# A mixture-of-experts block on one core: the third-largest expert gets 64 slots and whole weights, and its chunks alternate with the second split expert's

## The chip, the cores and the metric

The kernel runs on one core of a Trainium2 chip, the other cores being idle. The metric is the device time of one execution in microseconds (us), as the median of several runs. Five engines work side by side, each through its own queue in order: TensorE (PE in the profile; its weight loads are PEld), VectorE (DVE), ScalarE (ACT), GpSimd (POOL) and SyncE (SP), which here issues the loads from memory.

## The reference, cut to what matters

The program is a network of two layers over 256 tokens. Only the end of the second layer is touched: a mixture of eight experts, two chosen for each token.

```python
D_MODEL = 1024; SEQ = 256; N_EXPERTS = 8; TOP_K = 2; D_FF_EXPERT = 3584

def swiglu(h, w1, w3, w2):
    return (jax.nn.silu(h @ w1) * (h @ w3)) @ w2

def moe_swiglu(h, router, w1, w3, w2):
    logits = (h @ router).astype(jnp.float32)
    top_v, top_i = lax.top_k(logits, TOP_K)
    gates = jax.nn.softmax(top_v, axis=-1)
    dense_gate = jnp.sum(jax.nn.one_hot(top_i, N_EXPERTS, dtype=jnp.float32) * gates[..., None], axis=-2).astype(h.dtype)
    out = jnp.zeros_like(h)
    for e in range(N_EXPERTS):
        out = out + dense_gate[..., e:e + 1] * swiglu(h, w1[e], w3[e], w2[e])
    return out
```

All is float32. The weights of the eight experts are 352 MB and are read once from memory.

## The kernel before

**Places and slots.** The kernel numbers the experts by places p: place 0 is expert 0, places 1 to 7 are the other seven from the largest count of tokens to the smallest. `CAPS` gives each place its slots: 128, 192, 128, 128, 64, 64, 64, 64. Tokens beyond a place's slots would be worked off in a loop at the end of `moe`, which runs as often as there is an overflow.

**Chunks.** The 3584 hidden columns of an expert are cut into seven chunks of 512. A job (p, c) is one chunk c of place p. It has a first stage (`stage_a`), which multiplies the gathered tokens with a chunk of w1 and w3, a transposing step (`stage_t`, through PSUM bank `bk_po`), and a second stage (`stage_b`), which multiplies with a chunk of w2. The second stage of a job is written behind the first stage of the next one. A chunk uses six weight tiles of 128 x 2048 float32 (1 MB): four in its first stage, two in its second. The list `jobs` sets the order: all chunks of places 0, 2 and 3, then those of places 4 to 7, among which the seven chunks of place 1 are spread.

**Split and whole weights.** For places 0 to 3 a tile is split after it has landed: ScalarE copies it into a rounded half `hi` (L269) and VectorE subtracts that from the raw tile to get `lo` (L270). The tokens are split in the same way, and each product is three matmuls in the fast mode: hi by hi, hi by lo, lo by hi (L1554 to L1556). That gives 48 matmuls in a first stage and 24 in a second; below, such a chunk is called split. For places 4 to 7 the raw tile is used as it is, in float32, with 64 slots on one half of the array's columns, and two such matmuls run side by side on the two halves (L1551, L1763); these chunks are called whole, with 16 and 8 matmuls. The profile lists each of these matmuls as two. The results of a whole first stage lie in two halves of a PSUM bank, which ScalarE copies and VectorE adds (L1704 to L1709).

**Outputs.** A place's second stages add up in two PSUM banks over all seven chunks (`main`, bank `bk_mm`). Place 1, whose chunks are spread, uses two fresh banks for each block of slots and each chunk, and VectorE adds them up in SBUF, in the unused part of `xT` (`ysp`, L1860). At the last chunk `finish` scales the output and queues four scatter steps (L1815, L1816, bank `bk_ada`).

**Helper steps.** `prep_b`, `prep_c` and `prep_d` gather the tokens of later places, eight gather steps each (L1526). They and the scatter steps stand in a list `fills`, from which `stage_a` takes one after each weight tile.

**Loads.** Eleven slots of one tile each serve raw tiles and both halves of split ones. `plan` holds the loads in the order of use, `fetch` issues one (L1412, on SyncE's queue), `loaded` holds the raw tiles, `ready` those that were split or need no split. `prime` loads until `LEADS` (five in the steady state) tiles are in `loaded` and moves one on to `ready`, splitting it where it has to be; `next_w` calls it while `ready` holds no more than one tile. The instructions are then put in order by a scheduler, engine by engine, by the priority in which they were written and by what it thinks is free; the wait for a slot is part of that.

Of the kernel before, what the change touches and what calls it, by code (L numbers as in the profile page):

```python
# [10 lines left out]
F32 = mybir.dt.float32  # L11
# [7 lines left out]
P = 128  # L19
D = 1024  # L20
KD = 8
# [44 lines left out]
    return arrs, where  # L66


CAPS = (128, 192, 128, 128, 64, 64, 64, 64)
_CT, _CW = _const_tables()  # L70


# [95 lines left out]
def tile_backbone(ctx: ExitStack, tc: tile.TileContext, A, out, upto=99, dbg=None):  # L168
# [8 lines left out]
    AHEAD, LEAD, NWT, PRE, SPL = 1, 4, 11, (1, 3, 5, 7), (1, 3)  # L177
# [18 lines left out]
    def bank(tag="mm"):  # L196
        if turn and tag == "ax":
            turn.append(turn.pop(0))
            tag = turn[0]
        return ps[0].tile([P, 512], F32, tag=tag, name="bk_" + tag, bufs=NB[tag])  # L200
# [1207 lines left out]
    def load2(src, whole, parts=1):  # L1408
        raw = wtile(F32)
        dst, src = [a.rearrange("p (a b c) -> p a b c", a=2, b=parts) for a in (raw, src)]  # L1410
        for i in range(parts):
            nc.sync.dma_start(dst[:, :, i, :], src[:, :, i, :])  # L1412
        return raw, whole
# [12 lines left out]
    def prime():  # L1426
        lead[0] += 1
        n = LEADS[min(lead[0], len(LEADS) - 1)]
        while plan and len(loaded) < n:
            fetch()  # L1430
        ready.append(split2(*loaded.pop(0), SPC if lead[0] < NSPC else 2048))

    def next_w():
        while len(ready) <= AHEAD and (loaded or plan):
            prime()
        return ready.pop(0)

# [8 lines left out]

    jobs = []
    job = 0
    for p in (0, 2, 3, 4, 5, 6, 7):
        for c in range(7):  # L1450
            jobs.append((p, c))
            if p >= 4:
                if job in (1, 5, 9, 13, 17, 20, 23):
                    jobs.append((1, sum(j[0] == 1 for j in jobs)))
                job += 1
    ws = {}

    def w_get(p):
        if p not in ws:
            ws[p] = w_of(p)  # L1460
        return ws[p]

    for n in range(len(jobs) + 1):
        if n < len(jobs):
            for i in range(4):
                plan.append(lambda p=jobs[n][0], c=jobs[n][1], i=i: load2(w_get(p)[0](c, i), p >= 4))
        if n:
            for q in range(2):
                plan.append(lambda p=jobs[n - 1][0], c=jobs[n - 1][1], q=q, n=n: load2(w_get(p)[1](c, q), p >= 4,
                                                                                 2 if n == len(jobs) else 1))  # L1470

    def moe(mp, dw, oh0):
# [35 lines left out]
        def xg128():  # L1508
            return Pair(mp.tile([P, 2, KD, P], F32R, tag="xg", name="xg", bufs=4))
# [161 lines left out]
        def prep(specs, blocks, later):  # L1671
            oh = mk_oh(specs)
            ohT = mk_ohT(oh, specs)
            for k in range(KD):
                if later:
                    fills.append(lambda k=k: gather_k(oh, blocks, k))
                else:
                    gather_k(oh, blocks, k)
            return ohT
# [145 lines left out]
        def spec(p, base=0.0, gi=None, io=iota):  # L1825
            return (io, col(slp, p), base, col(gtp, p), p if gi is None else gi)


        def prep_b():
            xs[2], xs[3] = xg128(), xg128()  # L1830
            ohTs[2], ohTs[3] = prep([spec(2), spec(3)], [xs[2], xs[3]], True)

        def prep_c(a):
            t = mp.tile([P, 2, KD, 64], F32, tag="xg", name="xf", bufs=4)
# [8 lines left out]
        main = {}  # L1843

        def stage_2(p, c, gT):
            if p != 1:
                if c == 0:
                    main[p] = [[bank(), bank()]]
                stage_b(gT, main[p], c == 0, c == 6)
                if c == 6:  # L1850
                    finish(main[p][0], p, ohTs[p], p == 7)
                return
            acc = [[bank("ax"), bank("ax")] for _ in range(2)]
            stage_b(gT, acc, True, True)
            for b in range(2):
                for half in range(2):
                    if c == 0:
                        V.tensor_copy(ysp[b][half], two(acc[b][half]))
                    else:
                        V.tensor_tensor(ysp[b][half], ysp[b][half], two(acc[b][half]), op=ALU.add)  # L1860
            if c == 6:
                finish(ysp[0], 1, ohTs[1])
                finish(ysp[1], 8, ohTs[8])

        prev = None
        gT = []
        for p, c in jobs:
            if (p, c) == (0, 1):
                ohTs[0], = mk_ohT(oh0, [spec(0)])
                prep_b()  # L1870
            if (p, c) == (2, 1):
                prep_c(4)
            if (p, c) == (2, 3):
                prep_d()
            if (p, c) == (3, 1):
                prep_c(6)

            def mid():
                if prev is not None:
                    gT.append(stage_t(prev[1]))  # L1880

            gl = stage_a1(*a0) if prev is None else stage_a([xs[1], xs[8]] if p == 1 else [xs[p]], mid)
            if prev is not None:
                stage_2(*prev[0], gT.pop())
            prev = ((p, c), gl)
# [95 lines left out]
```

## Time and profile before

| | us |
|---|---|
| median of 3 runs | 2097.13 |
| lowest, highest | 2096.21, 2103.83 |
| profiled execution | 2096.44 |
| its span, first to last instruction | 2094.7 |
| busy: PE, PEld, DVE, ACT (whole span) | 2026.0, 1438.0, 1288.0, 906.0 |
| moved from memory | 493.4 MB |

The experts take the span from about 1123 us to its end. The profile comes from one execution; its times are us from the span's start. A busy share is an average over stages with different limits, so the stage has to be looked at by itself: there, the start of one matmul after another tells how long a piece takes (the listed duration of one overlaps with the next), and the idle time in square brackets at the end of a row, with the arrow, tells what the engine waited for.

### The profile page before, as it was taken

Reading aid. Unit: us, or ns where it says so; the run is one execution under the profiler, and the core shown is the slowest. Engines: PE = TensorE matmul, PEld = TensorE weight load, DVE = VectorE, ACT = ScalarE, POOL = GpSimd, SP = SyncE. Lnnn points to the kernel's source line nnn. Section 1 sums busy time; section 2 is a strip of 40 time slices with the busy share of each in tenths; the row PEclk is TensorE's granted clock in tenths of the full one; section 3 lists DMA queues with packets and bytes.
Section 4 is the critical chain, followed back from the end, with each engine's and each line's share of the span. In section 5 each row is a group of like instructions: output and inputs, shape, how many; then the busy total and the mean of one; then the engine's idle time right before and its main releaser. Section 6 shows DMA issues by size and latency. Waiting matters only on the chain. (4 is left out here: it accounts for less than half of the span.)

```text
span 2094.7 us, 26701 instructions
## 1 busy us (share of the span) xinstructions
PE 2026.0 (97%) x10170; PEld 1438.0 (69%) x10170; DVE 1288.0 (61%) x1878; ACT 906.0 (43%) x1296; POOL 109.1 (5%) x148
## 2 busy tenths in 40 slices
PE   7999999889999999999999999999999999999997
PEld 4776756688777878888888888878654554545453
DVE  5366557777566664765477888887644344434443
ACT  4346525643222223544356776767532232232322
POOL 0000015600000000100101000000000000000000
PEclk9999999999999999999999999999999999999998
DMA  8422432025444674322254999999989999999994
GB/s 317 150 94 96 151 121 95 24 68 161 142 150 151 209 236 128 125 61 81 84 228 146 337 364 323 322 334 335 371 352 397 401 406 398 390 418 383 384 361 181
DMA packets 89445, 496.25 MB, mean 237 GB/s; under 512 B 10080, under 2 KB 10848, under 8 KB 46048
## 3 DMA queue, kind: packets, MB, share of 16 engines
q1 hardware_dynamic: 89312, 494.49, 64.3%
q8 instruction: 82, 1.34, 0.3%
q14 instruction: 51, 0.42, 0.1%
HBM read 493.40 MB, written 1.05 MB: 236 GB/s over the span
## 5 line engine op out<-in xcount | busy, mean ns | idle before, releaser
L270 DVE TENSOR_TENSOR w<-w 128x2048 fp32r<-128x2048 f32 (+1 forms) x186 | 384.5, 2081 | 58.7 <-ACT w L269 40.9
L269 ACT ACTIVATE w<-w 128x2048 fp32r<-128x2048 f32 (+1 forms) x186 | 320.5, 1748 | 62.2 <-DVE w L270 35.4
L269 ACT ACTIVATE whi<-raw 128x1024 fp32r<-128x1024 f32 x151 | 160.0, 1060 | 404.1 <-PE bk_mm L298 263.3
L270 DVE TENSOR_TENSOR wlo<-raw,whi 128x1024 fp32r<-128x1024 f32 x151 | 186.6, 1236 | 140.8 <-ACT whi L269 138.3
L297 PE MATMUL bk_mm<-fH,whi 128*128 128x512 f32 (+1 forms) x360 | 140.0, 390 | 2.0 <-DVE xT L518 1.2
L299 PE MATMUL bk_mm<-fH,wlo 128*128 128x512 f32 (+1 forms) x360 | 138.8, 387 | 2.1 <-DVE wlo L270 2.1
L297 PE MATMUL bk_mm<-hH,whi 128*128 128x512 f32 (+1 forms) x384 | 137.5, 361 | 2.2 <-ACT hH L269 2.2
L298 PE MATMUL bk_mm<-fL,whi 128*128 128x512 f32 (+1 forms) x360 | 139.2, 388 | 0.0
L298 PE MATMUL bk_mm<-hL,whi 128*128 128x512 f32 (+1 forms) x384 | 136.2, 355 | 0.0
L299 PE MATMUL bk_mm<-hH,wlo 128*128 128x512 f32 (+1 forms) x384 | 135.5, 354 | 0.0
L1551 PE MATMUL bk_pt<-w,xf 128*64 128x512 f32 x448 | 113.0, 601 | 0.0
L1704 ACT COPY g<-bk_ax 64x512 f32<-64x512 f32 x35 | 20.4, 582 | 207.9 <-PE bk_ax L1551 207.7
L1551 PE MATMUL bk_ax<-w,xf 128*64 128x512 f32 x448 | 107.2, 597 | 0.0
L1763 PE MATMUL bk_mm<-w,gf 128*64 128x512 f32 x448 | 105.3, 597 | 0.0
L1555 PE MATMUL bk_ax<-w,xg 128*128 128x512 f32 x224 | 90.6, 405 | 7.2 <-DVE w L270 7.2
L1554 PE MATMUL bk_ax<-w,xg 128*128 128x512 f32 x224 | 89.6, 400 | 0.0
L1555 PE MATMUL bk_pt<-w,xg 128*128 128x512 f32 x220 | 88.5, 402 | 0.4 <-DVE w L270 0.2
L1556 PE MATMUL bk_ax<-w,xg 128*128 128x512 f32 x224 | 88.8, 396 | 0.0
L456 POOL TENSOR_TENSOR rstd<-rstd,mhalf 128x2 f32<-128x2 f32 (+2 forms) x11 | 10.3, 937 | 1496.1 <-DVE rstd L455 1477.0
L1554 PE MATMUL bk_pt<-w,xg 128*128 128x512 f32 x220 | 88.2, 401 | 0.0
L1556 PE MATMUL bk_pt<-w,xg 128*128 128x512 f32 x220 | 87.5, 398 | 0.0
L297 PEld LDWEIGHTS bk_mm<-hH,whi 128*128 128x128 f32 x384 | 71.8, 188 | 21.8 <-issue 5.4
(568 smaller groups left out, 4357.4 us busy)
## 6 DMA issues: line engine op xcount, KB each, us to landing
w<-in_m SPq DMA_DIRECT2D x334, 1024.0 KB, 7.6
raw<-in_f SPq DMA_DIRECT2D x66, 512.0 KB, 3.7
araw<-in_adc SPq DMA_DIRECT2D x56, 512.0 KB, 3.9
araw<-in_ada SPq DMA_DIRECT2D x32, 512.0 KB, 7.2
raw<-in_evx SPq DMA_DIRECT2D x29, 512.0 KB, 3.7
raw<-in_odx SPq DMA_DIRECT2D x22, 512.0 KB, 3.6
raw<-in_evo SPq DMA_DIRECT2D x12, 512.0 KB, 3.7
xT<-in_xt SPq DMA_DIRECT2D x4, 1024.0 KB, 6.4
```

Of the source, the lines that this page charges most:

```text
L269: a = S.activation(hi, src, AF.Copy)
L270: v = V.tensor_tensor(lo, src, hi.bitcast(F32), op=ALU.subtract)
L297: T.matmul(o, wh, xh, start=first, stop=False)
L298: T.matmul(o, wh, xl, start=False, stop=False)
L299: T.matmul(o, wl, xh, start=False, stop=last)
L456: G.tensor_tensor(r, r, mhalf[:, :n], op=ALU.pow)
L1551: T.matmul(o[c:c + 64], sl(b[0]), wh, start=k < 2, stop=k >= K - 2, tile_position=(0, c))
L1554: T.matmul(o, sl(b[0]), wh, start=first, stop=False)
L1555: T.matmul(o, sl(b[0]), wl, start=False, stop=False)
L1556: T.matmul(o, sl(b[1]), wh, start=False, stop=last)
L1704: S.copy(g[0:64], hb[b][0][64:128])
L1763: T.matmul(accs[0][half][64 * q2:64 * q2 + 64], gT[0][0][:, f, :], wh[:, hs], start=first and q == 0, stop=last and q == 1, tile_position= ...
```

## The change

Place 3 gets 64 slots and whole weights (`p >= 3` in `load2`, `spec` with `iotd`, a float32 token tile of 64 columns). Its chunks no longer follow those of place 2 but alternate with them, chunk by chunk. Its output adds up in SBUF as that of place 1 does, in the first block of `ysp`, which is free until place 1 begins. The gathers of places 6 and 7 (`prep_c(6)`) start at job (4, 1). `prime` now counts the tiles in `ready` too (six in all), and `next_w` goes on past whole tiles, up to four, until a split tile is in `ready`, so that a split can be written up to four tiles ahead of its use.

```diff
-CAPS = (128, 192, 128, 128, 64, 64, 64, 64)
+CAPS = (128, 192, 128, 64, 64, 64, 64, 64)
...
     def prime():
         lead[0] += 1
         n = LEADS[min(lead[0], len(LEADS) - 1)]
-        while plan and len(loaded) < n:
+        while plan and (not loaded or len(loaded) + max(len(ready), 1) < n + 1):
             fetch()
         ready.append(split2(*loaded.pop(0), SPC if lead[0] < NSPC else 2048))
 
     def next_w():
-        while len(ready) <= AHEAD and (loaded or plan):
+        while (len(ready) <= AHEAD or len(ready) < 4 and not any(w[1] is not None for w in ready)) and (loaded or plan):
             prime()
         return ready.pop(0)
...
-    for p in (0, 2, 3, 4, 5, 6, 7):
+    for p in (0, 2, 4, 5, 6, 7):
         for c in range(7):
             jobs.append((p, c))
+            if p == 2:
+                jobs.append((3, c))
...
-                plan.append(lambda p=jobs[n][0], c=jobs[n][1], i=i: load2(w_get(p)[0](c, i), p >= 4))
+                plan.append(lambda p=jobs[n][0], c=jobs[n][1], i=i: load2(w_get(p)[0](c, i), p >= 3))
...
         def prep_b():
-            xs[2], xs[3] = xg128(), xg128()
-            ohTs[2], ohTs[3] = prep([spec(2), spec(3)], [xs[2], xs[3]], True)
+            xs[2], xs[3] = xg128(), [mp.tile([P, KD, 64], F32, tag="xg", name="xf", bufs=4)]
+            ohTs[2], ohTs[3] = prep([spec(2), spec(3, io=iotd)], [xs[2], xs[3]], True)
...
         def stage_2(p, c, gT):
-            if p != 1:
+            if p not in (1, 3):
...
-            acc = [[bank("ax"), bank("ax")] for _ in range(2)]
+            acc = [[bank("ax"), bank("ax")] for _ in gT]
             stage_b(gT, acc, True, True)
-            for b in range(2):
+            for b in range(len(gT)):
...
             if c == 6:
-                finish(ysp[0], 1, ohTs[1])
-                finish(ysp[1], 8, ohTs[8])
+                for b in range(len(gT)):
+                    finish(ysp[b], (p, 8)[b], ohTs[(p, 8)[b]])
...
-            if (p, c) == (3, 1):
+            if (p, c) == (4, 1):
                 prep_c(6)
```

The order of VectorE before, in one chunk of place 3 (`w` are weight tiles with their buffer number: `lo<-raw,hi`; `gl` is the lower half of the transposed hidden chunk, L1701 the product for the next one):

```order
L1701 TENSOR_TENSOR g_12233<-g_12233,bk_pt_12151 128x512
L270 TENSOR_TENSOR w_12239<-w_12152,w_12238 128x2048
L270 TENSOR_TENSOR w_12257<-w_12170,w_12256 128x2048
L270 TENSOR_TENSOR gl_12326<-bk_po_12320,gh_12325 128x512
L270 TENSOR_TENSOR w_12277<-w_12197,w_12276 128x2048
L270 TENSOR_TENSOR w_12305<-w_12215,w_12304 128x2048
L270 TENSOR_TENSOR w_12332<-w_12236,w_12331 128x2048
L270 TENSOR_TENSOR w_12350<-w_12254,w_12349 128x2048
```

The order of VectorE now, from the end of a first stage of place 2 through the chunk of place 3 that follows (the lines of the changed kernel lie two further on: L1703, L1743 for L1701, L1741):

```order
L1703 TENSOR_TENSOR g_11558<-g_11558,bk_pt_11482 128x512
L1862 TENSOR_TENSOR xT_72<-xT_72,bk_ax_11561 128x2x256
L1862 TENSOR_TENSOR xT_72<-xT_72,bk_pt_11562 128x2x256
L1707 TENSOR_TENSOR g_11612<-g_11612,bk_ax_11577 64x512
L270 TENSOR_TENSOR gl_11601<-bk_po_11595,gh_11600 128x512
L270 TENSOR_TENSOR w_11588<-w_11569,w_11587 128x2048
L1710 TENSOR_TENSOR g3_11613<-g3_11613,bk_pt_11578 64x512
L1711 TENSOR_TENSOR g_11612<-g_11612,g3_11613 64x512
L1743 COPY gf_11703<-bk_po_11698 128x256
L270 TENSOR_TENSOR w_11627<-w_11579,w_11626 128x2048
L270 TENSOR_TENSOR w_11645<-w_11585,w_11644 128x2048
```

The six subtractions of a pair of chunks stand as one (`w_11588`, the first tile of place 2's second stage) and five behind `gf` (`w_11627` is the second tile, `w_11645` the first of the next first stage); before, each pair had twelve.

The order of TensorE before, in the second stage of a chunk of place 3, at the change from its first tile (`w_12217`, `w_12218`) to its second (`w_12238`, `w_12239`):

```order
L1555 MATMUL bk_mm_11691<-w_12218,gh_12193 128x512
L1556 MATMUL bk_mm_11691<-w_12217,gl_12194 128x512
L1554 MATMUL bk_mm_11690<-w_12238,gh_12193 128x512
L1554 MATMUL bk_mm_11691<-w_12238,gh_12193 128x512
L1738 MATMUL bk_po_12320<-ca_67,g_12233 128x128 x4
L1555 MATMUL bk_mm_11690<-w_12239,gh_12193 128x512
L1556 MATMUL bk_mm_11690<-w_12238,gl_12194 128x512
```

And now, in the second stage of a chunk of place 2, at the same change of tiles:

```order
L1557 MATMUL bk_mm_10556<-w_11588,gh_11600 128x512
L1558 MATMUL bk_mm_10556<-w_11587,gl_11601 128x512
L1740 MATMUL bk_po_11698<-ca_67,g_11612 128x64 x4
L1556 MATMUL bk_mm_10555<-w_11626,gh_11600 128x512
L1556 MATMUL bk_mm_10556<-w_11626,gh_11600 128x512
L1557 MATMUL bk_mm_10555<-w_11627,gh_11600 128x512
L1558 MATMUL bk_mm_10555<-w_11626,gl_11601 128x512
```

The transposes of place 3's chunk now stand between the two tiles, and what VectorE needs from them (`gf`) stands ahead of the subtraction that gives `w_11627`.

The order of TensorE now, in a first stage of place 2 just behind its first tile (`w_11644`, `w_11645`):

```order
L1558 MATMUL bk_ax_11660<-w_11644,xg_9496 128x512
L1556 MATMUL bk_ax_11660<-w_11664,xg_9496 128x512
L1765 MATMUL bk_ax_11740<-w_11642,gf_11703 64x512
L1557 MATMUL bk_ax_11660<-w_11665,xg_9496 128x512
L1558 MATMUL bk_ax_11660<-w_11664,xg_9496 128x512
```

Matmuls of place 3's second stage (L1765) are set in among those of place 2's first: one here, two behind the second tile, five at the end. Before, no second stage was cut up in this way in the chunks of places 2 and 3.

## Rows read from the trace of the kernel before

**Rows 1.** Windows: length; busy us by engine; PEclk, DMA share, GB/s.

```profile
1243.60:1506.30 262.70, 261.15 (x1211) 210.72 (x1210) 219.89 (x156) 182.06 (x162) 0.00 (x0) 1.00 0.94 335
1506.30:1538.60 32.30, 31.81 (x136) 13.97 (x134) 14.30 (x20) 12.79 (x13) 0.00 (x0) 1.00 1.00 413
1538.60:2069.00 530.40, 516.06 (x2318) 265.43 (x2316) 224.44 (x266) 151.45 (x170) 0.00 (x0) 1.00 0.95 384
```

**Rows 2.** Waits of PE, 1243.6 to 1506.3: total us, times, longest.

```profile
PE bk_ax L1555 <- DVE w L270: 1.2, 2, 0.6
```

**Rows 3.** Timeline of PE, one split chunk: start, us, engine, line, operation, tiles.

```profile
1226.28 0.40 PE L1554 MATMUL bk_ax<-w,xg 128*128 128x512 f32 x1
...
1237.52 0.63 PE L1554 MATMUL bk_mm<-w,gh 128*128 128x512 f32 x2
...
1243.58 0.39 PE L1554 MATMUL bk_ax<-w,xg 128*128 128x512 f32 x1
```

**Rows 4.** Timeline of PE, one whole chunk and the next one's start.

```profile
1660.30 3.65 PE L1551 MATMUL bk_ax<-w,xf 128*64 128x512 f32 x16
1663.89 0.46 PE L1738 MATMUL bk_po<-ca,g 64*128 64x64 f32 x4
1664.28 3.65 PE L1551 MATMUL bk_pt<-w,xf 128*64 128x512 f32 x16
1667.76 3.60 PE L1763 MATMUL bk_mm<-w,gf 128*64 128x512 f32 x16
1671.19 1.89 PE L1551 MATMUL bk_ax<-w,xf 128*64 128x512 f32 x8
```

**Rows 5.** Timeline of PE, single whole matmuls among split ones.

```profile
1497.79 1.07 PE L1551 MATMUL bk_ax<-w,xf 128*64 128x512 f32 x2
1498.79 0.51 PE L1555 MATMUL bk_pt<-w,xg 128*128 128x512 f32 x1
...
1504.84 1.08 PE L1551 MATMUL bk_ax<-w,xf 128*64 128x512 f32 x4
1505.85 0.50 PE L1555 MATMUL bk_mm<-w,gh 128*128 128x512 f32 x1
```

**Rows 6.** Timeline of all engines, a whole chunk ahead of place 1's second stage.

```profile
1643.95 0.66 PE L1738 MATMUL bk_po<-ca,g 128*128 128x128 f32 x4
...
1644.54 1.93 PE L1551 MATMUL bk_pt<-w,xf 128*64 128x512 f32 x6
...
1645.40 0.63 ACT L1706 ACTIVATE g<-g 64x512 f32<-64x512 f32 x1
...
1647.18 1.90 ACT L269 ACTIVATE w<-w 128x2048 fp32r<-128x2048 f32 x1
...
1649.11 2.29 DVE L270 TENSOR_TENSOR w<-w 128x2048 fp32r<-128x2048 f32 x1 [1.37 <-ACT w L269]
...
1651.46 0.50 PE L1555 MATMUL bk_ax<-w,gh 128*128 128x512 f32 x1 [0.98 <-DVE w L270]
```

**Rows 7.** Timeline of all engines, from transposes over `gf` to a subtraction.

```profile
1615.33 0.43 PE L1738 MATMUL bk_po<-ca,g 64*128 64x64 f32 x4 [0.49 <-DVE g L1709]
...
1615.68 1.08 PE L1763 MATMUL bk_mm<-w,gf 128*64 128x512 f32 x4
1615.79 0.42 DVE L1741 COPY gf<-bk_po 128x256 f32<-128x256 f32 x1 [0.61 <-PE bk_po L1738]
1616.13 2.28 DVE L270 TENSOR_TENSOR w<-w 128x2048 fp32r<-128x2048 f32 x1
```

**Rows 8.** DMA, 1500 to 2070, in 40 slices; issues, KB each, median us to landing.

```profile
GB/s 380 408 372 225 423 333 423 418 419 420 360 412 421 416 367 420 342 421 419 418 420 316 415 420 421 417 420 350 423 403 368 290 415 420 314 420 325 405 419 194
...
w<-in_m SPq DMA_DIRECT2D x206, 1024.0 KB, 10.2
```

**Rows 9.** Waits of PE, 1538.6 to 2069: total us, times, longest.

```profile
PE bk_ax L1555 <- DVE w L270: 10.9, 12, 2.1
```

**Rows 10.** The additions in SBUF, by source line: ns min, median, max.

```profile
L1860 DVE TENSOR_TENSOR xT<-xT,bk_ax x12: 678/683/690, 1658.8 to 2029.7; 128x512 f32<-128x512 f32 x12
```

## What the change will do to the time: a prediction

> **What bounds the kernel now.** I began with the table of stretches. From 1243.6 to 1506.3 us the chunks of the second split expert (p = 2) and then of the third-largest (p = 3) run; in these 262.7 us TensorE is busy for 261.2, while the loads move 335 GB/s [rows 1]. The waits of TensorE there come to 1.2 us in two places [rows 2]. So this stretch is bound by TensorE's own work, and the copies, subtractions and loads stand behind it. A split chunk without helper steps takes 17.30 us: 11.24 for the 48 matmuls of its first stage and 6.06 for the 24 of its second with four transposes (1226.28, 1237.52, 1243.58) [rows 3]. Fourteen make 242.2, which leaves 20.5 us for the 32 helper steps of the stretch (4 + 4 scatter steps of `finish`, 8 + 8 + 8 gathers of `prep`): 0.64 us each. In the last stretch the loads are nearly the bound too: 384 GB/s over 530 us [rows 1], against 420 in its best slices [rows 8]; a tile of 1.049 MB then takes 2.50 us. The clock is full in all three stretches [rows 1].
>
> **The third-largest expert with 64 slots.** Its 55 tokens fit: counted from the reference's inputs the router gives the eight experts 87, 39, 55, 145, 15, 52, 18 and 101, and 55 is the third behind expert 0, so the overflow loop stays empty. A whole chunk needs 7.46 us for the first stage with its transposes (1660.30 to 1667.76) and 3.43 for the second (to 1671.19) [rows 4], 10.9 in place of 17.3: 6.4 saved per pair of chunks if nothing else moved. Its 42 tiles also need no copy (1.90) and no subtraction (2.29) [rows 6]; these were hidden behind TensorE and are worth nothing by themselves. The output now adds two VectorE operations of 0.68 per chunk [rows 10]; VectorE was busy for 219.9 of 262.7 [rows 1] and loses 42 subtractions, so they hide.
>
> **One pair of chunks, by the new order.** Between the first matmul of one p = 2 chunk and the next, TensorE now runs: 48 split matmuls, 11.24; inserted into them, whole matmuls of the p = 3 second stage, first one alone, then two, at the end five. One alone takes 1.00 (1497.79 to 1498.79), two 1.01 (1504.84 to 1505.85) [rows 5]; five are three turns of 0.86 (3.43 / 4), 2.58. With 0.1 for each way back that is 4.9 where eight together took 3.43. Then the whole first stage, 7.46, whose transposes are the larger ones here (0.59 in place of 0.39 [rows 4, 6]), 7.66; then the split second stage, 6.06 with 0.35 in place of 0.44 for its transposes [rows 3, 7], and 0.15 to change over. Sum: **29.9**. Loads for 12 tiles need 30.0 at best, no more than this.
>
> Two waits come on top, both read from the order of VectorE and ScalarE. (1) The split of the first second-stage tile stands behind ScalarE's silu of the whole chunk. In rows 6 the same sequence runs: from the start of the transposes (1643.95) the silu ends after 2.08 (1645.40 + 0.63); a copy and subtraction follow, 1.93 to the subtraction's start and 2.35 more until TensorE goes on (1647.18, 1649.11, 1651.46): 6.4 in all. TensorE arrives after 0.59 + 3.48 (second half of the whole stage) + 0.15 + 0.47 (two matmuls that need the copy alone): 4.7. **Wait 1.7.** (2) The subtraction of the second tile stands behind `gf`, which needs the transposes that TensorE does between the two tiles. From their start to the split's it is 0.80 (1615.33, 1615.79, 1616.13) [rows 7], and 2.35 until TensorE goes on: 3.15. TensorE is there after 0.35 + 0.47. **Wait 2.3.** Behind the waiting matmul all of TensorE's queue stands still. The other four subtractions follow at 2.3 each, faster than the 2.8 of the 12 matmuls that use one; no third wait. The slots for the loads free early enough: the first raw tile of the next pair is issued when the third split tile is used up, some 17 us before its copy. So a pair takes **33.9 us, against 34.6 before**: seven pairs save 4.9, not 45. Bounds for a pair: 30.0, if both waits vanish, and 38.4, if copy and subtraction (1.93 + 2.35) are exposed in full twice. I take 33.9, since both sequences stand in the rows.
>
> **Helper steps.** Twenty of the 32 remain in the stretch, 20 x 0.64 = 12.8. In four places the order puts such steps, or the next expert's whole matmuls, exactly where wait (2) is, and that fills 4 x 2.3 = 9.2. The first pair has expert 0's last split second stage instead of a whole one, 6.06 for 4.9: 1.2 more, and single whole matmuls stand among split ones, about 3 (three of 1.00, an estimate from rows 5). 12.8 + 1.2 + 3 - 9.2 = 7.8 in place of 20.5: **12.7 saved**. Twelve steps move behind 1506.3 (gathers of the last two experts, scatter of p = 2): +7.7; the last p = 3 second stage is whole now, -2.6; three of the gathers stand where the first p = 1 chunk made TensorE wait for a split, up to 2.1 [rows 9], -1.6: **+3.5**.
>
> **The chunks of the largest expert (p = 1), seven of them.** Their first stage is now cut by one and by three whole matmuls, about 1.4 more each. Against that, the split of their first second-stage tile moves ahead of the transposes' `gl` on VectorE, which removes a wait of about 1.2 (one half of the 10.9 us in 12 waits [rows 9] and the gap before 1651.46 [rows 6]), and one set of transposes goes from among the whole matmuls to the split ones, 0.5. Net -0.3 x 7 = **-2**, with ends of -7 (all waits of rows 9 gone) and +8 (the cuts cost, nothing is won, as the loads hold the stretch).
>
> **Sum.** -4.9 - 12.7 + 3.5 - 2 = -16.1. The profiled execution took 2096.4 (span 2094.7 and 1.7 around it), so 2080.3; the median of the three runs shown is 0.7 higher: **2081**.
>
> **Rivals.** (a) *The loads eat it.* With the second stretch shorter, everything rests on the last one, where loads run at 384 of 420 GB/s: the steps moved there cost in full (+2.6 and +1.6) and p = 1 comes out at +8 in place of -2: 2081 + 14 = 2095. For it: a long landing time, 10.2 us in the middle [rows 8]. Against it: TensorE's waits there are for VectorE [rows 9], not for a load.
> (b) *Slower.* Copy and subtraction are exposed in full at both places of every pair, because the slot of the copied half or the raw tile is not there when ScalarE's turn comes: 38.4 per pair, 31 more in seven; the four filled places give back some 8: 2104. It takes over from the kernel before at 36.2 per pair. Against it: in rows 6 the copy starts as soon as ScalarE is free.
> (c) *The earlier splitting does what its rule says* (up to four tiles ahead, past whole ones) and neither wait appears: 30.0 per pair, bound by the loads, 27 less; the filled places then win nothing, +9: 2063. Against it: the order, where the subtraction stands behind `gf`.
> (d) *Loads capped lower.* Twelve tiles would then set the pair. The slices of 420 GB/s and the mean of 384 over 530 us speak against any cap below [rows 1, 8]. The Trainium skill, "DMA: Bandwidth & Descriptors", section "Where 436 GB/s comes from", lets the memory side bind such loads at about 358 GB/s per core; by that a pair would take 12.58 MB / 358 = 35.1, and seven some 8 more: 2089. Here one core runs alone, and the trace exceeds that figure; the measurement decides.
>
> **How the numbers follow.** About 0.5% (10.5 us) is what a measurement of this kernel can tell from no change. Chances: the forecast 0.50, with a spread of its own of 2072 to 2091, three quarters of it below 2086.6; (a) 0.26; (b) 0.11; (c) 0.10; (d) 0.03. Faster: 0.38 + 0.10 = 0.48; slower: 0.11; the same: 0.41. The range must take in half of (c) and stop before (b): 2064 to 2100 leaves out about 2 in 10.
>
> **What would show it.** Right: the distance between first matmuls of two p = 2 chunks is 33 to 35 us without helper steps; in each pair TensorE waits twice for VectorE's subtraction, for about 1.7 and 2.3; loads in the stretch run near 370 GB/s. Wrong: waits of 4 at these places (b); waits on loads, or landing times over 10 us in the second stretch (a, d); no waits and 30 us (c). If the last stretch changes by more than 8 us, the p = 1 term was mis-sized.

## The result: slower by 0.9%, and where the time went

The changed kernel takes 2118.31 us (median of 5 runs, 2115.46 to 2121.98) against 2097.13 of before (median of 5): ratio 1.0088, 95% interval 1.0074 to 1.0103. The forecast was 2081, with a range from 2064 to 2100; the time moved the other way.

The stretches of the changed kernel, cut at the first matmul of each chunk of place 2, then at the first and the last chunk of place 1 (columns as in [rows 1]: length; busy us by engine; PEclk, DMA share, GB/s):

```profile
1238.97:1280.57 41.60, 39.89 (x177) 26.34 (x176) 26.43 (x27) 19.48 (x22) 0.00 (x0) 0.96 0.82 315
1280.57:1324.61 44.04, 39.44 (x170) 23.51 (x169) 22.57 (x27) 18.23 (x26) 0.00 (x0) 0.93 0.73 286
1324.61:1366.15 41.54, 36.50 (x150) 21.46 (x148) 20.96 (x24) 16.65 (x21) 0.00 (x0) 0.91 0.77 304
1366.15:1400.92 34.77, 31.38 (x134) 17.67 (x133) 19.10 (x16) 14.77 (x14) 0.00 (x0) 1.00 0.91 362
1400.92:1436.04 35.12, 31.73 (x130) 17.76 (x128) 18.78 (x15) 14.98 (x12) 0.00 (x0) 0.97 0.90 359
1436.04:1472.46 36.42, 33.03 (x130) 18.81 (x129) 18.51 (x14) 14.74 (x12) 0.00 (x0) 0.93 0.87 346
1472.46:1546.64 74.18, 69.75 (x297) 32.85 (x295) 33.07 (x47) 19.09 (x29) 0.00 (x0) 1.00 0.89 354
1546.64:2007.72 461.08, 446.27 (x1972) 228.19 (x1972) 187.53 (x215) 133.80 (x153) 0.00 (x0) 0.99 0.94 377
```

The same two stretches of the kernel before, from the first matmul of (2, 0) to that of (1, 0) and from there to (1, 6):

```profile
1243.58:1538.65 295.07, 293.03 (x1345) 224.71 (x1343) 234.19 (x176) 194.88 (x175) 0.00 (x0) 1.00 0.95 343
1538.65:1985.25 446.60, 435.29 (x1963) 224.35 (x1961) 186.34 (x214) 130.20 (x144) 0.00 (x0) 1.00 0.96 391
```

Of the changed kernel's rows, the first six are pairs of chunks. Only the fourth looks like the forecast of 33.9; the first three, which hold the helper steps (but for one gather in the fourth), take over 41, and five of the six have a PEclk below 1, where [rows 1] had 1.00 throughout. By stretch, in us:

| stretch | before | forecast | after |
|---|---|---|---|
| start to the first matmul of (2, 0) | 1243.6 | 1243.6 | 1239.0 |
| (2, 0) to (1, 0) | 295.1 | 281.0 | 307.7 |
| (1, 0) to (1, 6) | 446.6 | 444.6 | 461.1 |
| (1, 6) to the end of the span | 109.5 | 109.5 | 108.4 |

The forecast column takes -4.9 - 12.7 + 3.5 off the second stretch and 2 off the third. What lies ahead of (2, 0) differs by up to 7 us between profiled executions, also where this part is written the same (1245.0 and 1238.0 in the two kernels e3 and e14 below), so from here on times are counted from (2, 0). From there the change costs 26.0 us, of which 12.6 come before (1, 0), 14.5 between (1, 0) and (1, 6), and -1.1 after.

The waits of TensorE, 1118 to 2090 us (total us, times, longest):

```profile
PE bk_mm L1557 <- DVE w L270: 14.8, 10, 2.1
PE bk_po L1740 <- DVE g L1711: 5.4, 11, 0.5
PE bk_ax L1557 <- DVE w L270: 4.5, 7, 1.6
PE bk_ada L1528 <- DVE xs1b L1542: 4.0, 3, 1.3
PE bk_mm L1765 <- DMA w<-in_m: 3.5, 3, 1.2
PE bk_ada L1528 <- ACT xf L1538: 3.3, 6, 0.6
```

The largest row before, over the same stretch:

```profile
PE bk_ax L1555 <- DVE w L270: 12.1, 14, 2.1
```

The first row of the changed kernel is new and is the two waits of the forecast: the second stages of place 2 (`bk_mm`) wait for VectorE's subtraction. The gathers (`bk_ada`, L1528), which had no row of this kind before, now wait for their own evacuation, and whole second stages of the last stretch wait for a load. The six rows come to 35.5 us, the longest wait to 2.1.

In the fourth pair, which has the full clock of 2.4 GHz (PEclk 1.00), ScalarE, VectorE and TensorE at the two places:

```profile
1388.48 1.90 ACT L269 ACTIVATE w<-w 128x2048 fp32r<-128x2048 f32 x1
...
1390.41 2.29 DVE L270 TENSOR_TENSOR w<-w 128x2048 fp32r<-128x2048 f32 x1 [1.86 <-ACT w L269]
...
1392.76 0.50 PE L1557 MATMUL bk_mm<-w,gh 128*128 128x512 f32 x1 [1.34 <-DVE w L270]
...
1395.79 0.42 DVE L1743 COPY gf<-bk_po 128x256 f32<-128x256 f32 x1 [1.78 <-PE bk_po L1740]
1396.13 4.48 DVE L270 TENSOR_TENSOR w<-w 128x2048 fp32r<-128x2048 f32 x2
...
1398.47 0.50 PE L1557 MATMUL bk_mm<-w,gh 128*128 128x512 f32 x1 [2.05 <-DVE w L270]
```

The copy (behind the silu) ends, the subtraction follows, TensorE goes on after a wait of 1.34; then `gf`, the next subtraction and a wait of 2.05. The forecast had 1.7 and 2.3.

In the second pair, TensorE through two gather steps and the second stage behind them, with three rows of ScalarE and VectorE:

```profile
1314.65 0.74 PE L1528 MATMUL bk_ada<-oh,hTok 128*128 128x256 f32 x4 [0.78 <-DVE ohT L1664]
1315.42 0.37 ACT L1538 ACTIVATE xg<-bk_ada,mod 128x128 fp32r<-128x128 f32 x1 [6.09 <-PE bk_ada L1528]
...
1315.88 1.91 ACT L269 ACTIVATE w<-w 128x2048 fp32r<-128x2048 f32 x1
...
1316.72 0.71 PE L1528 MATMUL bk_ada<-oh,hTok 128*128 128x256 f32 x4 [1.33 <-DVE xs1b L1542]
1317.83 2.29 DVE L270 TENSOR_TENSOR w<-w 128x2048 fp32r<-128x2048 f32 x1 [1.25 <-ACT w L269]
1317.85 0.99 PE L1556 MATMUL bk_mm<-w,gh 128*128 128x512 f32 x2 [0.42 <-ACT w L269]
1320.17 0.79 PE L1557 MATMUL bk_mm<-w,gh 128*128 128x512 f32 x1 [1.34 <-DVE w L270]
1320.77 0.63 PE L1558 MATMUL bk_mm<-w,gl 128*128 128x512 f32 x1
1321.19 0.63 PE L1557 MATMUL bk_mm<-w,gh 128*128 128x512 f32 x1
...
1324.61 0.57 PE L1556 MATMUL bk_ax<-w,xg 128*128 128x512 f32 x1
```

A gather's results are taken out of PSUM by ScalarE and then by VectorE (L1538, L1542). In ScalarE's queue that stands ahead of the copy of a second-stage tile: ScalarE is idle for 6.09 us until the gather comes, and copies the tile only then, at 1315.88. TensorE waits four times: 0.78 ahead of the first gather, 1.33 until VectorE has taken out its result, 0.42 for the copy and 1.34 for the subtraction. Then the clock is at its lower level, 1.2 GHz: matmuls start 0.42 apart (0.23 in the fourth pair), and from the wait to the next stage the piece takes 4.44 us (1320.17 to 1324.61) where the same piece in the fourth pair takes 2.45 (1398.47 to the next stage at 1400.92).

### The profile page after: what moved, and what is told of

It reads as the page before. It is cut to its first block, busy times and chain, and to the rows that moved or that the text cites. A ratio compares the mean times of both kernels' runs of the same rounds, so it can differ in the third digit from the quotient of the medians.

```text
span 2116.1 us, 26245 instructions
## 1 busy us (share of the span) xinstructions
PE 2022.4 (96%) x10002; PEld 1372.9 (65%) x10002; DVE 1209.2 (57%) x1856; ACT 831.5 (39%) x1261; POOL 110.1 (5%) x148
## 3 DMA queue, kind: packets, MB, share of 16 engines
q8 instruction: 81, 1.33, 0.3%
## 5 line engine op out<-in xcount | busy, mean ns | idle before, releaser
L270 DVE TENSOR_TENSOR w<-w 128x2048 fp32r<-128x2048 f32 (+1 forms) x144 | 289.2, 2022 | 118.1 <-ACT w L269 74.6
L269 ACT ACTIVATE w<-w 128x2048 fp32r<-128x2048 f32 (+1 forms) x144 | 240.5, 1697 | 80.0 <-PE bk_mm L1765 39.3
L1553 PE MATMUL bk_ax<-w,xf 128*64 128x512 f32 x560 | 138.9, 596 | 0.0
L1553 PE MATMUL bk_pt<-w,xf 128*64 128x512 f32 x560 | 134.1, 598 | 0.0
L1765 PE MATMUL bk_mm<-w,gf 128*64 128x512 f32 x448 | 113.9, 600 | 3.5 <-DMA w<-in_m 3.5
L1553 PEld LDWEIGHTS bk_ax<-w,xf 128*64 128x64 f32 x560 | 40.9, 137 | 73.7 <-issue 71.9
L297 PEld LDWEIGHTS bk_mm<-fH,whi 128*128 128x128 f32 x360 | 68.0, 189 | 22.5 <-issue 3.6
L1553 PEld LDWEIGHTS bk_pt<-w,xf 128*64 128x64 f32 x560 | 38.4, 136 | 67.2 <-issue 64.7
L298 PEld LDWEIGHTS bk_mm<-hL,whi 128*128 128x128 f32 x384 | 72.2, 188 | 13.2 <-issue 3.4
L299 PEld LDWEIGHTS bk_mm<-fH,wlo 128*128 128x128 f32 x360 | 68.2, 190 | 17.2 <-DVE wlo L270 2.3
L299 PEld LDWEIGHTS bk_mm<-hH,wlo 128*128 128x128 f32 x384 | 72.2, 188 | 10.8 <-issue 1.6
```

What stands on the lines that cost most here:

```text
L269: a = S.activation(hi, src, AF.Copy)
L270: v = V.tensor_tensor(lo, src, hi.bitcast(F32), op=ALU.subtract)
L297: T.matmul(o, wh, xh, start=first, stop=False)
L298: T.matmul(o, wh, xl, start=False, stop=False)
L299: T.matmul(o, wl, xh, start=False, stop=last)
L1553: T.matmul(o[c:c + 64], sl(b[0]), wh, start=k < 2, stop=k >= K - 2, tile_position=(0, c))
```

## Experiments

Each ratio is to runs of the kernel before on the same chip (their medians were 2101.1 to 2102.3). A stretch is read from one profiled execution each. The theories came from the traces above: W, that whole chunks among split ones stall TensorE; L, that the new loading rule costs the last stretch (rival M: that this came from what ran ahead of it); H, that gathers stall it among whole chunks; and for each stall, that the half clock behind it adds to it.

**e1: the loading rule of before in the changed kernel.**

```diff
-        while plan and (not loaded or len(loaded) + max(len(ready), 1) < n + 1):
+        while plan and len(loaded) < n:
...
-        while (len(ready) <= AHEAD or len(ready) < 4 and not any(w[1] is not None for w in ready)) and (loaded or plan):
+        while len(ready) <= AHEAD and (loaded or plan):
```

> The changed kernel with the loading rule of before (prime and next_w as they were), all else as changed. Theory L (the rule costs the last stretch: a tile split early holds two slots, so later loads start late): from the first matmul of chunk (1, 0) to that of (1, 6) it goes back from 461.1 us to about 447, as before, and the total falls by 12 to 15, to about 2104. Theory M (the last stretch lost by what the change put at its start, twelve helper steps and a stalled TensorE at half clock): that distance stays at 458 to 462 and the total at about 2118. Either way the pairs of chunks of places 2 and 3 are no better than 34.3 to 36 us each without helper steps, since their waits for the subtraction come from the order and not from the rule; if the rule does help there, as it was written to, they get longer by 1 to 3 and the total rises by up to 15.

Measured: 2124.85, ratio 1.011 (1.0088 to 1.0131). A clean pair, and the stretch from (1, 0) to (1, 6):

```profile
1409.60:1446.80 37.20, 32.95 (x129) 19.18 (x128) 18.73 (x14) 14.61 (x12) 0.00 (x0) 0.91 0.87 344
1564.00:2016.70 452.70, 439.37 (x1961) 227.09 (x1960) 185.76 (x213) 131.65 (x145) 0.00 (x0) 0.99 0.94 384
```

The second takes 452.7 in place of 461.1, so L holds for 8.4 of the 14.5 us; 6.1 stay without the rule, as M would have it. The pairs take 37.2, over 2 more than the fifth pair of the changed kernel (1.2 of it in busy time, at a clock of 0.91 in place of 0.97), and (2, 0) to (1, 0) takes 319.4. The rule does help in the pairs, and harms behind them.

**e2: the new loading rule alone, in the kernel before** (the two lines above the other way round).

> The kernel before with only the new loading rule. Theory L: the distance from (1, 0) to (1, 6), 446.6 us before, grows by 8 to 14 and the total to 2105 to 2111; the split chunks of places 0, 2 and 3 stay at 17.3 us, since no whole tile stands among them. Theory M: no change, 2095 to 2099.

Measured: 2107.31, ratio 1.0031 (1.0016 to 1.0047). From (2, 0) to (1, 0) it takes 296.1; the stretch from (1, 0) to (1, 6):

```profile
1536.50:1996.60 460.10, 443.38 (x1963) 224.75 (x1962) 188.34 (x217) 130.42 (x144) 0.00 (x0) 0.99 0.95 380
```

Two rows of TensorE's waits, 1118 to 2090:

```profile
PE bk_ax L1555 <- DVE w L270: 7.3, 9, 2.7
PE bk_mm L1763 <- DMA w<-in_m: 6.0, 4, 2.6
```

The first stretch is unchanged, the second 13.5 us longer than before's 446.6. The waits for the subtraction fall from 12.1 to 7.3 us, as the rule means to, and 6.0 us of waits for a load appear, with 380 GB/s in place of 391. That is less than half of the 13.5: TensorE is also busy for 8.1 us longer with as many matmuls (443.4 against 435.3), at a clock of 0.99. That a tile split early takes two slots, which later loads then lack, fits the waits for loads, but was not measured by itself. L is shown: the rule costs by itself. M is not refuted by it; e1 leaves it 6 us.

**e3: place 3 with 64 slots and whole weights (`load2` and `prep_b` as in the change), but behind place 2 as before, output in PSUM, loading rule of before.**

```diff
-CAPS = (128, 192, 128, 128, 64, 64, 64, 64)
+CAPS = (128, 192, 128, 64, 64, 64, 64, 64)
...
-                plan.append(lambda p=jobs[n][0], c=jobs[n][1], i=i: load2(w_get(p)[0](c, i), p >= 4))
+                plan.append(lambda p=jobs[n][0], c=jobs[n][1], i=i: load2(w_get(p)[0](c, i), p >= 3))
...
```

> The kernel before with place 3 in whole weights and 64 slots, but its chunks behind those of place 2 as before, its output in PSUM as before, the loading rule of before. Theory W (the whole weights save TensorE's time, and the alternation gives it back in waits for subtractions and in the half clock behind them): place 3's seven chunks take 15 us each, the time of six loads at 2.50, in place of 17.3, so 2097 - 16 = 2081; if the loads run ahead in place of waiting, down to 2060. The rival (whole weights are worth nothing since the loads are the bound of all that follows): 2093 to 2099.

Measured: **2068.37, ratio 0.9849 (0.983 to 0.9868)**. Its chunks of place 2, then the stretch from (3, 0) to (1, 0):

```profile
1245.00:1370.80 125.80, 125.11 (x598) 102.29 (x597) 106.21 (x87) 89.27 (x87) 0.00 (x0) 1.00 0.92 327
1370.80:1508.65 137.85, 127.95 (x580) 50.84 (x579) 42.11 (x64) 31.09 (x52) 0.00 (x0) 1.00 1.00 412
```

The second holds nine whole chunks, 15.3 each, at 412 GB/s with the DMA engines always busy: bound by the loads, with the helper steps hidden in them. The gain over before, 31 us from (2, 0) to (1, 0), is twice the 16 expected: in a stretch whose length the loads set, the helper steps add nothing. So the whole weights are worth 1.5%, and the rest of the change lost more than that.

**e5: ScalarE's order in the whole chunks of place 3.** The copies of place 2's two second-stage tiles go ahead of those of the whole chunk's results (`cut` lists the splits; the split of the transposed tile and the copy to `g3` are held back in the same way):

```diff
+                    if early and i == 1 and q == 1:
+                        prime()
                     wh, wl = next_w()
...
+                    with tc.issue_after(cut[-2 if early else -1][0]) if early else nullcontext():
-                    S.copy(g[0:64], hb[b][0][64:128])
+                        S.copy(g[0:64], hb[b][0][64:128])
...
```

> The changed kernel with one thing in the order: in the whole chunks of place 3, ScalarE's copies of the first and the second second-stage tile of place 2 stand ahead of the copies of the whole chunk's own results, so their subtractions come earlier. Theory W: TensorE's waits for the subtraction in the second stages of place 2 (14.8 us in 10 waits over the experts) fall below 5, the clock no longer falls in the last four pairs, these take 30 to 32 us in place of 34.3 to 36.4, and the total falls by 15 to 25, to 2093 to 2103. The rival (the pairs are bound by their loads, and the waits only cover that): TensorE waits for landings instead, pairs stay above 34, total 2112 to 2118.

Measured: 2114.66, ratio 1.0078 (1.0053 to 1.0103), not below the changed kernel beyond the interval. A row of ScalarE at the first tile:

```profile
1422.47 1.91 ACT L269 ACTIVATE w<-w 128x2048 fp32r<-128x2048 f32 x1 [9.61 <-DMA w<-in_m]
```

Two rows of TensorE's waits, 1118 to 2090, and the last pair:

```profile
PE bk_ax L1558 <- DVE w L270: 14.3, 12, 2.3
PE bk_mm L1558 <- DVE w L270: 6.7, 5, 1.6
...
1435.70:1470.00 34.30, 32.01 (x130) 18.29 (x129) 18.61 (x14) 14.15 (x11) 0.00 (x0) 0.95 0.91 366
```

The waits in the second stages fall from 14.8 to 6.7, but the first stages now wait, 14.3 in place of 4.5: the stall moved to the later tiles, and the copy that stands first waits for its raw tile to land. The last two pairs still take 34.6 and 34.3 us. But they do so at a clock of 0.95: in the last one TensorE is idle for 2.3 us, against 3.4 in e13's pairs of the same length below, and busy for 1.1 longer. So the order did shorten the waits, and the clock took it back; what such a pair would take at full clock no run shows. The rival's time came true, but not its reason: TensorE waits for subtractions, not for landings.

**e6: alternation alone, all weights split.** The kernel before with the new `jobs`, `stage_2` and `prep_c(6)` at (4, 1).

> The kernel before with only the order of the chunks changed: place 3's chunks alternate with place 2's, its output is added up in SBUF, the last gathers start at (4, 1), but its weights stay split with 128 slots and the loading rule stays. Theory W (TensorE stalls because whole chunks stand among split ones: six tiles in a row need splitting, then none): all tiles are split at an even pace here, so no new waits, seven pairs of 34.6 us and helper steps at 0.64; from the first chunk of place 2 to (4, 0) it takes 253 to 265, the total is 2095 to 2103. The rival (alternating costs by itself, through the cut-in second stages and the additions): 2108 to 2120.

Measured: 2110.91, ratio 1.0042 (1.0026 to 1.0059), where the theory had 2103 at most. From (2, 0) to the first whole matmul of (4, 0), and from there to (1, 0):

```profile
1241.20:1488.70 247.50, 246.81 (x1131) 199.33 (x1129) 217.45 (x156) 175.74 (x144) 0.00 (x0) 1.00 0.96 344
1488.70:1548.20 59.50, 52.96 (x217) 27.52 (x217) 26.80 (x40) 16.27 (x25) 0.00 (x0) 0.91 0.75 292
```

Before, these took 254.2 and 40.9:

```profile
1497.80:1538.65 40.85, 40.36 (x168) 19.38 (x167) 19.17 (x23) 14.04 (x14) 0.00 (x0) 1.00 0.98 395
```

So alternating costs next to nothing by itself: the first stretch runs at full clock with one wait of 0.6 and is 6.7 shorter, where the twelve helper steps that left were priced at 7.7. The loss sits where these went: 18.6 us for the nine of them that stand ahead of (1, 0) (four scatter steps and five gathers; three gathers follow behind), some 2 each, and the clock at 0.91. Before (1, 0) TensorE there does one gather after another:

```profile
1539.47 0.74 PE L1528 MATMUL bk_ada<-oh,hTok 128*128 128x256 f32 x4 [0.61 <-ACT xf L1538]
1540.81 1.20 PE L1528 MATMUL bk_ada<-oh,hTok 128*128 128x256 f32 x4 [0.61 <-ACT xf L1538]
1542.62 1.22 PE L1528 MATMUL bk_ada<-oh,hTok 128*128 128x256 f32 x4 [0.61 <-ACT xf L1538]
```

From the second of these rows on the clock is at its lower level: a gather takes 1.20 in place of 0.74, and the next one starts 1.81 later in place of 1.34.

**e7: eight gathers earlier.** The changed kernel with:

```diff
-            if (p, c) == (2, 1):
+            if (p, c) == (0, 3):
                 prep_c(4)
-            if (p, c) == (2, 3):
+            if (p, c) == (2, 1):
                 prep_d()
```

> The changed kernel with the gathers of places 4 and 5 written at chunk (0, 3) in place of (2, 1), and those of place 1 at (2, 1) in place of (2, 3). Theory H (a gather step costs more between whole matmuls, since its two evacuations stand behind the splitting on ScalarE and VectorE and TensorE waits for them, which brings the half clock as well; among the split chunks of place 0 it costs 0.64): the three pairs that hold the gathers take 127 us together in place of 104 for three without, 23 for 20 steps; with eight of them gone the stretch falls by 7 to 12, place 0 grows by 5, and the total falls by 2 to 8, to 2110 to 2116. The rival (a step costs the same everywhere): 2117 to 2120.

Measured: 2109.52, ratio 1.0037 (1.0024 to 1.0051): 8.8 below the changed kernel (0.51% by the ratios), a little more than expected. The six pairs take 216.3 in place of 233.5. H holds.

**e9: place 2's second stage ahead of place 3's first stage, loading rule of before.** The plan of loads and the main loop go a(2, c), b(3, c-1), b(2, c), a(3, c):

```diff
+            own = stage_t(gl) if p == 2 else None
+            if prev is not None and prev[0][0] != 2:
                 stage_2(*prev[0], gT.pop())
+            if p == 2:
+                stage_2(p, c, own)
```

> The chunks alternate as in the changed kernel, with the loading rule of before, but the second stage of place 2 stands ahead of the first stage of place 3 and not behind it, so that the tiles to split come as four and two with whole ones between, and not as six in a row. Theory W (the run of six is what VectorE and ScalarE can't follow): pairs without helper steps take 30 to 33 us in place of 37.2 with that loading rule, from (1, 0) to (1, 6) 447 to 453, total 2085 to 2105. The rival (slots or loads bound the pairs): 34 to 38 a pair, total 2112 to 2128.

Measured: 2133.11, ratio 1.0146 (1.0125 to 1.0166). The pairs without helper steps take 37.7 and 37.9, no better than the 37.2 of e1; the first of them:

```profile
1414.70:1452.40 37.70, 33.76 (x129) 18.50 (x129) 18.25 (x14) 14.15 (x12) 0.00 (x0) 0.91 0.82 323
```

So the run of six split tiles is not what sets a pair. The waits for subtractions moved again to the first stages (21.4 us in 17), and the clock is at 0.91 in both pairs, as in e1.

**e10: e9 with the gathers of e7.**

> As e9_own_b_first, with the gathers early as in e7_gathers_early. Theory H: 3 to 9 below e9_own_b_first. The rival: within 2 of it.

Measured: 2122.95, ratio 1.0099 (1.0082 to 1.0116), 10.2 below e9: H again, in another order of the chunks.

**e11: e3 with place 1's chunks spread over 35 whole chunks** (`if p >= 3` and `job in (1, 6, 11, 16, 21, 26, 30)`).

> As e3_whole_in_a_row, with the seven chunks of place 1 spread over the 35 whole chunks of places 3 to 7 in place of the 28 of places 4 to 7. Theory W: in a row, place 3's chunks wait for their loads (15.4 us each at 412 GB/s for 10.9 of TensorE's work), while the last stretch is bound by both; a split chunk among them uses the idle time, so the total falls by 5 to 20 below e3_whole_in_a_row, to 2048 to 2063. The rival (the loads are at their bound in both stretches, so their order is worth nothing): within 4 of it.

Measured: 2093.35, ratio 0.9967 (0.9954 to 0.9979): 25 above e3, where neither side had it. At the start of a chunk of place 1 ScalarE has this row:

```profile
1514.30 1.91 ACT L269 ACTIVATE w<-w 128x2048 fp32r<-128x2048 f32 x1 [5.02 <-DMA w<-in_m]
```

ScalarE was idle for 5.02 us until the raw tile landed, so no load was ahead there any more, and copy and subtraction stand open; TensorE waits 2.63 for the copy, and the mean clock from (1, 1) on is 0.96 and 0.97 in the next two stretches. So here the idle time of TensorE that loads leave was not time in which split chunks could be put; that the other places lose by the same row was not followed up.

**e12: e7 with the last eight gathers at (0, 5)** (places 3 to 5 share a pool slot for that).

> As e7_gathers_early (alternating, the new loading rule), with the gathers of places 6 and 7 written at (0, 5) in place of (4, 1); the tokens of places 3 to 5 share one slot of the pool to make room. Theory H (eight gathers in a lump ahead of the first chunk of place 1 stall TensorE, 0.6 us each behind their evacuation, and let the clock fall): from (4, 0) to (1, 0) it takes 46 us in e7 and 34 to 39 here, place 0 grows by 5, and the total falls by 2 to 8 below e7_gathers_early, to 2101 to 2108. The rival (the load of that chunk's first tiles is what comes late, and the gathers only fill the time): from (4, 0) to (1, 0) no shorter than 43, total 2108 to 2116.

Measured: 2098.19, ratio 0.9982 (0.9969 to 0.9995), 11.3 below e7 (0.55% by the ratios), more than expected. From the seventh chunk of place 2 to (1, 0), where five of the eight gathers stood, it takes 64.2 in place of e7's 74.3; from (1, 0) to (1, 6), where the other three stood, 455.1 in place of 463.6. H holds for these eight too, and what ran at the start of the last stretch did cost it time, as M said.

**e13: e12 with the new loading rule in places 2 and 3 alone** (the condition in `prime` is bound to `pairs` in the same way)**.**

```diff
-        while (len(ready) <= AHEAD or len(ready) < 4 and not any(w[1] is not None for w in ready)) and (loaded or plan):
+        while (len(ready) <= AHEAD or pairs[0] and len(ready) < 4 and not any(w[1] is not None for w in ready)) and (loaded or plan):
...
+            pairs[0] = p in (2, 3)
```

> As e12_gathers_all_early, with the new loading rule in the chunks of places 2 and 3 alone and the rule of before elsewhere. Theory L (the rule costs 8 to 14 us in the last stretch, as e1 and e2 show): from (1, 0) to (1, 6) 447 to 453, total 8 to 14 below e12_gathers_all_early. The rival (that stretch depends on what runs ahead of it): within 4 of it. If H and L both hold, this is the alternation at its best, some 2092 to 2098: no faster than the kernel before, and 25 slower than the same whole weights in a row.

Measured: **2089.88, ratio 0.9946 (0.993 to 0.9962)**, 8.3 below e12 (0.36% by the ratios), and faster than before, where I had expected a draw. Its first two pairs, with eight gathers and the scatter steps, take 41.6 and 37.2. The third to the sixth (the middle two left out), then the way to (1, 0), then (1, 0) to (1, 6):

```profile
1332.10:1366.40 34.30, 30.91 (x130) 17.20 (x129) 18.64 (x14) 14.19 (x12) 0.00 (x0) 1.00 0.92 367
...
1435.00:1469.30 34.30, 30.91 (x130) 17.20 (x129) 18.64 (x15) 14.17 (x12) 0.00 (x0) 1.00 0.93 368
1469.30:1533.50 64.20, 62.36 (x266) 28.40 (x264) 33.50 (x44) 20.17 (x21) 0.00 (x0) 1.00 0.97 392
1533.50:1978.90 445.40, 435.35 (x1963) 224.47 (x1961) 184.63 (x213) 130.22 (x144) 0.00 (x0) 1.00 0.97 392
```

Four pairs of exactly 34.30 at full clock; (2, 0) to (1, 0) in 280.2, (1, 0) to (1, 6) in 445.4, 9.7 less than in e12: L again.

**e14: e3 with the gathers written at (3, 1), (3, 3) and (3, 5).**

> As e3_whole_in_a_row, with the gathers of places 4 and 5, of place 1 and of places 6 and 7 written at (3, 1), (3, 3) and (3, 5) in place of (2, 1), (2, 3) and (3, 1). Theory B (place 2's chunks are bound by TensorE, where a gather step costs 0.64; place 3's by the loads, where it costs nothing): sixteen steps leave the first and the total falls by 7 to 11 below e3_whole_in_a_row. The rival, after e7 (gathers among whole chunks stall TensorE at their evacuation and the clock falls with it): the same or up to 8 above it.

Measured: 2066.99, ratio 0.9851 (0.9829 to 0.9873), the same as e3. Place 2 takes 117.3 in place of 125.8, the stretch behind it 152.9 in place of 137.9: sixteen steps that cost 8.5 among split chunks cost more among whole ones that wait for loads. The rival is right. e3 and e14 are the fastest versions of all; e13, e12 and e11 also lie below the kernel before, by 0.5% and less.

## Why the prediction was wrong, point by point

**The pair of chunks: right.** 33.9 forecast, 34.3 measured at full clock (e13, and the fourth pair here at 34.77, with one gather in it). The rows split it into 30.91 of work (29.9 in the sum) and two waits of 1.34 and 2.05 (1.7 and 2.3), at the places and for the reasons that the order gave. That the sum is off by 0.4 only is partly luck: the work came out 1.0 longer and the waits 0.6 shorter. Rival (c), no waits, is out; so is (b), waits of 4; (d) too, since e13's pairs load at 368 GB/s and e3's whole chunks at 412. The Trainium skill, "DMA: Bandwidth & Descriptors", section "Where 436 GB/s comes from", gives some 358 GB/s for such loads; both rates here are above it.

**The helper steps: the step that failed first.** The sum had 20 steps at 0.64 in the pairs, less 9.2 for waits that they fill, plus 4.2 for the first pair: 7.8 in all. The first three pairs take 127.2 against 3 x 34.3, so 24.3. The step that failed is "exactly where wait (2) is, and that fills". The waits for the subtraction in the second stages did shrink, to 3.3 us in these three pairs from 3 x 3.39; but the helper steps and the copies held up behind them brought some 8 us of other waits, and TensorE is idle for 11.3 of the 127.2 (lengths less busy times in the first three rows), where three clean pairs have 10.2. So filling won nothing in place of 9.2. TensorE's busy time grew by 23.1 (115.8 against 3 x 30.91): some 8.5 of it is the clock (below), and the 14.6 that are left are no more than the 17.0 that the steps and the first pair were priced at. So 0.64 was right as the work of a step where split matmuls cover its evacuation, and wrong as its price next to a wait: its evacuation stands in the two queues that the wait is for, ahead of what TensorE waits for. e7 took eight steps out: 17.2 less in the pairs, while (2, 0) came 7.4 later, with those steps in place 0.

**The steps moved behind 1506.3: the same mistake.** +7.7 for twelve in the sum, and -1.6 for three of them that were to fill a wait at (1, 0). e6 shows 18.6 for the nine ahead of (1, 0), 5.4 of it by the clock (59.5 x 0.09). e12 gets 10.1 back for five, and 8.5 behind (1, 0), where the three had been.

**The last stretch: mis-sized by 16.5.** -2 forecast, with ends of -7 and +8; measured +14.5. The loading rule was treated as acting on the pairs, and on place 1 only as a saved wait. e2 shows it alone at +13.5; taking it out of the stretch gives back 8.4 (e1) or 9.7 (e13 against e12). The other part came from what ran ahead: 6.1 stay in e1 without the rule, and 8.5 go in e12 with the gathers. In the changed kernel the waits for the subtraction there fell from 7.9 us to 3.9, about half of the 1.2 x 7 that was forecast; against it stand 3.5 of waits for loads and 2.8 for ScalarE's copies, which the sum did not have, and TensorE is busy for 11.0 longer (446.3 against 435.3, three gathers more). Rival (a), "the loads eat it", had the direction, but its +8 has no clock in it and no waits of gathers at (1, 0).

**The clock: missing from the sum.** The prediction noted that it was full and priced every wait by its length. Length times (1 - PEclk) over the rows of the changed kernel gives 12.1 us in the pairs (1.7 + 3.1 + 3.7 + 1.1 + 2.5) and some 5 in the last stretch: up to 17 of the 26 us, if TensorE had work all that time, and overlapping with the terms above rather than added to them. Between runs of one kernel the time follows the clock: e13's eight runs go from 2084.81 us at a mean clock of 0.994 to 2095.83 at 0.989, and of e7's ten one takes 2102.10 at 0.991 and another 2113.46 at 0.984.

**Put together.** From the changed kernel to e13 the time falls by 8.8 (e7), 11.3 (e12) and 8.3 (e13), from 2118.3 to 2089.9. Each number is the difference to the run before, so that they add up proves nothing; that each change brought a fall clear of its intervals does. In e13 (2, 0) to (1, 0) takes 280.2 and (1, 0) to (1, 6) 445.4, where the forecast had 281.0 and 444.6; that they agree so closely is partly chance, since sixteen gathers sit in place 0 there and make it about 10 longer. The forecast priced the alternation and the whole weights, and left out what stalls do to the clock, what a helper step does to the queues that it needs, and what the loading rule does elsewhere.

**Why even that is not the best.** A pair of 34.3 stands against 17.3 + 15.3 = 32.6 in a row (e3), where split chunks have full cover and whole ones run at the pace of the loads, with the helper steps hidden.

## What to carry to other kernels

Price a moved helper step by what it waits for at its new place, not by its duration at the old one: if its result is taken out by the engines that the wait is for, it holds up their queues and brings waits of its own. A rule for loads or buffers acts wherever it is called, so put the stretch that it was not written for into the sum, and try the rule alone. When a change brings short waits to an engine that had none, price them together with the clock that they may cost.

## What the runs showed of the hardware

TensorE's clock fell although no single wait in the pairs was longer than 2.1 us; in e6 it fell behind two waits of 0.61 between gathers. Pairs three to six of e12 have the same matmuls in the same order, and each has the same two waits, of 1.34 and 2.05:

```profile
1332.70:1366.90 34.20, 30.81 (x129) 17.15 (x128) 18.64 (x14) 12.63 (x12) 0.00 (x0) 1.00 0.93 368
1366.90:1402.00 35.10, 31.71 (x129) 17.78 (x128) 18.77 (x15) 14.97 (x12) 0.00 (x0) 0.98 0.90 359
1402.00:1438.50 36.50, 33.11 (x129) 18.86 (x128) 18.51 (x14) 14.83 (x12) 0.00 (x0) 0.93 0.87 346
1438.50:1472.80 34.30, 30.91 (x129) 17.20 (x128) 18.64 (x14) 12.72 (x12) 0.00 (x0) 1.00 0.92 367
```

With the clock at 1.00 they take 34.2 and 34.3, with it at 0.98 and 0.93 they take 35.1 and 36.5. The Trainium skill, "TensorE: Matmul & The Clock Gate", section "HAM oscillation — how this bites in real kernels", describes a kernel whose waits for loads, between bursts of matmuls, let the clock fall again and again. The trace here agrees that it falls and rises again within one kernel; the waits in that description are longer than any in these pairs, so that waits of 2.1 us and less go with a falling clock is what the trace here adds. What decides whether it falls in one pair and not in the next stays open: no run here tells it.
